# Expert weights in 18 places instead of 17, three of them loaded in the merge, and merged rows split into two halves per token tile

## The chip, the cores and the metric

The kernel runs on one core of a Trainium2 chip. The metric is the device time of one execution in microseconds (us), as the median of several executions. The engines are TensorE (PE, its weight loads PEld), VectorE (DVE), ScalarE (ACT), GpSimd (POOL) and SyncE (SP); SP issues nearly all plain DMAs, POOL the indirect ones.

## The reference

One decoder layer for 1024 tokens of 1024 channels in float32. A combined input projection feeds two token mixers (a native sparse attention with 8 heads and an attention over a latent with 8 heads). Their outputs are projected, merged with per-channel gates, projected once more and added to the input; a layer norm gives `h`. Then every token goes to two of 32 experts, and a second layer norm ends the layer.

```python
g_sel = argmax(h @ w_grp + b_grp)                  # one of 4 groups
e_logits = (h @ w_rtr + b_rtr)[group g_sel]        # 8 experts in it
top_l, top_i = lax.top_k(e_logits, 2)
...
y = (silu(x @ w_gate[e]) * (x @ w_up[e])) @ w_down[e]
out = layer_norm(ALPHA * h + sum of weight * y, ln2_g, ln2_b)
```

D_MODEL is 1024, the inner width of an expert 256, so an expert's three matrices are 3 MB in float32, and all 32 are 96 MB.

## The kernel before

**Precision.** Every float32 operand of a matmul is split into a high and a low part of a shorter type (`split`, lines 59 and 60: ACT casts the high part, DVE subtracts it for the low part), and three matmuls high*high, high*low, low*high stand for one.

**Stages.** Input projections (line 204); attention, head by head (lines 465 to 660); the merge (`merge_part`, line 711: for each block `dt` of 128 output channels, PE multiplies the two mixers' outputs by `w_br`, DVE multiplies by the gate, line 715, and adds the two, line 752); the output projection (line 978, eight tiles of 128 tokens, each followed by its layer norm, its router logits and the store of `h` into `h_d`); the routing tail, which makes the table `tkv` of the tokens of each expert; 32 experts, one after the other; the final norm.

**Before, merged rows.** For each `dt` the sum of line 752 is 128 channels by 1024 tokens. It is split at once into `MH`, four pairs of a high and a low tile with 256 tokens each. They lie in slots 9 to 16 of 8 KB a partition, all eight slots, and stay there until the output projection has read them as stationary operands.

**Slots.** On-chip memory is kept as numbered slots of 8 KB a partition, whose tiles take turns. Expert weights come in 96 loads of 1 MB (128 partitions by 8 KB) through `prefetch`, line 813; each load takes the next place of the list `RING`, 17 places in turn with `last` as the seventeenth. 16 loads are called for between the tiles of the output projection, when the places of `MH` come free, the others when an earlier expert has used its place. From load 18 on, a load waits until the load four before it has landed:

```python
            if n >= 18:
                tc.add_manual_dep(d, loads[n - 4].name, sync, reason="few loads in flight")
```

SP issues in the order of its instruction list; behind the 17th load it reads `novi` (line 1161), which the routing tail makes, and only then goes on.

**An expert** (class `Expert`, line 1020 on) takes a gather of its tokens from `h_d` (POOL, lines 1043 and 1046), eight transposes of them (`turn`, line 1063) and their split, four `up` steps (line 1086, each with a weight tile of 128x1024 split by `parts`, lines 1073 and 1074: ACT casts, DVE subtracts), SiLU times the second half (`act`, lines 1091 and 1092), a transpose (`flip`, line 1097), two `down` steps (line 1109, with two more split weight tiles), the scaling with the routing weight (ACT line 1112, DVE line 1113), and an indirect add into `acc_d` (POOL, line 1114). The six split weight tiles of an expert go in turn through slots 18, 19 and 20. PE's order in the experts is written by hand; the order of ACT, DVE, POOL and SP is decided when the kernel is built, by a scheduler with its own estimates of time. A moved address or load can therefore change the order of instructions elsewhere.

Of the kernel before, what the change touches and what calls it, by code (L numbers as in the profile page):

```python
# [18 lines left out]
P = 128  # L19
T = 1024  # L20
D = 1024
# [23 lines left out]
def layer_kernel(ctx: ExitStack, tc: tile.TileContext, A, out, dbg=None):  # L45
# [12 lines left out]
    def split(h, l, src):  # L58
        S.copy(h, src)  # L59
        V.tensor_tensor(l, src, f(h), op=ALU.subtract)  # L60
# [379 lines left out]
    def slot(j, shape, dt=F32):  # L440
        return (u1 if j < 5 else u3 if j < 7 else u2).tile(shape, dt, name=f"slot{j}", tag=f"slot{j}")
# [290 lines left out]
    aw0s.close()  # L732
    ats.close()

    hp = ctx.enter_context(tc.tile_pool(name="hp", bufs=1))
    u2 = ctx.enter_context(tc.tile_pool(name="u2", bufs=1))
    rp = ctx.enter_context(tc.tile_pool(name="rp", bufs=1, side="right"))
    with tc.tile_pool(name="mg", bufs=1, side="right") as mg:
        MH = [(slot(9 + 2 * q, [P, KD, 256], F32R), slot(10 + 2 * q, [P, KD, 256], F32R)) for q in range(4)]
        merge_part("a", 0)  # L740
        merge_weights(1, rp)
        merge_weights(2, rp)
        merge_part("b", 0)
        for dt in range(KD):
            if dt + 1 < KD:
                merge_part("a", dt + 1)
            if dt > 0:
                merge_part("b", dt)
            if dt + 3 < KD:
                merge_weights(dt + 3, rp)  # L750
            ga, gb = GV["a"].pop(0), GV["b"].pop(0)
            V.tensor_tensor(ga, ga, gb, op=ALU.add)
            for q in range(4):
                split(MH[q][0][:, dt], MH[q][1][:, dt], ga[:, q * 256:(q + 1) * 256])


    tkv = hp.tile([P, NE, 2], I32, name="tkv")
# [18 lines left out]
    def normalize(r, gb, pool, kind, nb, junk):  # L776
# [18 lines left out]
        else:  # L795
            S.activation(r, r, AF.Identity, scale=rs, bias=mv[:, 1:2])
            V.tensor_tensor(r, r, gb[:, 0], op=ALU.mult)
            (V if kind in "xy" else G).tensor_tensor(r, r, gb[:, 1], op=ALU.add)


    RING = [5, 6, 7, 7, 17, 9, 10, 11, 12, 13, 14, 15, 16, 1, 2, 0]
    weights, loads = [], []
    sync = mybir.DependencyInfo(mybir.DependencyClass.Sync, mybir.DependencyReason.DATA)

    def prefetch(n=1):
        for _ in range(min(n, 3 * NE - len(weights))):
            e, c = divmod(len(weights), 3)
            n = len(weights)
            if n == 2:
                pair["x"] = u0.tile([P, 2, 2, D], F32, name="ring7", tag="slot7")  # L810
            r = n % 17
            t = pair["x"][:, r - 2] if r in (2, 3) else ep.tile([P, 2, D], F32, name="last", bufs=1) if r == 16 else slot(RING[r], [P, 2, D])
            d = nc.sync.dma_start(flat(t), A["w_ex"][TURN[e], :, c * 2048:(c + 1) * 2048]).ins
            if n >= 18:
                tc.add_manual_dep(d, loads[n - 4].name, sync, reason="few loads in flight")
            loads.append(d)
            weights.append(t)

    with tc.tile_pool(name="wo", bufs=1, side="right") as wo, tc.tile_pool(name="wo2", bufs=2, side="right") as wo2:
        WO = []  # L820
# [146 lines left out]
        for i in range(NT):  # L967
            ts = slice(i * P, (i + 1) * P)
            s = ps.tile([P, T], F32, name="s")
            last = i == NT - 1  # L970
            xr = rp.tile([P, D], F32, name="wr", bufs=3)
            nc.sync.dma_start(xr, A["x"][ts])
            bs = wo2.tile([P, 2, 6], F32, name="bs")
            for cs in ((0,), (1,)) if last else ((0, 1),):
                for k in range(KD):
                    for x, (a, b) in enumerate(((0, 0), (0, 1), (1, 0))):
                        for c in cs:
                            mm = PE.matmul(s[:, HALF[c]], MH[i // 2][a][:, k, (i % 2) * P:(i % 2) * P + P],  # L978
                                           WO[k][:, b, HALF[c]], start=(k == 0 and x == 0),
                                           stop=(k == KD - 1 and x == 2)).ins  # L980
                cc = slice(512 * cs[0], 512 * cs[-1] + 512)
                V.scalar_tensor_tensor(xr[:, cc], xr[:, cc], ALPHA, s[:, cc], op0=ALU.mult, op1=ALU.add)
                for c in cs:
                    V.bn_stats(bs[:, c], xr[:, HALF[c]])
            mv, rs = moments(bs, wo2, 2)
            if last:
                with tc.issue_after(mm):
                    logits(hT, lt, range(KD))
                held = gather(i - 1, lt)
            hT = wo2.tile([P, T], F32, name="hT", bufs=1)  # L990
            lt = ps.tile([P, 512], F32, name="pt")
            for cs in ((0,), (1,)) if last else ((0, 1),):
                cc = slice(512 * cs[0], 512 * cs[-1] + 512)
                with tc.issue_after(done) if cs == (1,) else nullcontext():
                    done = scale(xr[:, cc], gb1[:, :, cc], mv, rs)
                for c in cs:
                    t = transposed([xr[:, k * P:(k + 1) * P] for k in range(4 * c, 4 * c + 4)])
                    S.copy(hT[:, HALF[c]], t)
            if i != NT - 2:
                logits(hT, lt, range(KD))  # L1000
            nc.sync.dma_start(h_d[ts], xr)
            kept.append(nc.sync.dma_start(acc_d[ts], xr).ins)
            if last:
                with tc.issue_after(done):
                    route(*held)
            if i != NT - 2:
                g = gather(i, lt)
                if g:
                    route(*g)
            prefetch({0: 5, 1: 2, 3: 2, 5: 2, 7: 5}.get(i, 0))  # L1010


        pp = ps.tile([P, 512], F32, name="pv")[:, 0:32]
# [148 lines left out]
    with tc.For_i(0, nov, 1) as j:  # L1162
# [10 lines left out]
        x.fetch()  # L1173
        x.turn()
        for c in range(3):
            x.w[c] = slot(RING[9 + c], [P, 2, D])
            nc.sync.dma_start(flat(x.w[c]), src[:, c * 2048:(c + 1) * 2048])
            if c < 2:
                x.up(4 * c)
                x.up(4 * c + 2)  # L1180
# [2 lines left out]
        x.down()  # L1183


    gb2 = slot(RING[8], [P, 2, D])
    for x, n in enumerate(("ln2_g", "ln2_b")):
        d = nc.sync.dma_start(gb2[:, x], A[n].partition_broadcast(P)).ins
        tc.add_manual_dep(d, loads[-1].name, sync, reason="not ahead of the experts")
    junk = slot(RING[9], [P, 2, D])[:, 0]  # L1190
    R = [t[:, x] for t in (slot(j, [P, 2, D]) for j in RING[4:8]) for x in range(2)]
    for i in range(NT):
        d = nc.sync.dma_start(R[i], acc_d[i * P:(i + 1) * P]).ins
        for o in Expert.sums:
# [96 lines left out]
def _program(shapes, extra=None):  # L1291
    import concourse.bacc as bacc

    nc = bacc.Bacc("TRN2", target_bir_lowering=False, num_devices=1)
    A = {n: nc.dram_tensor(f"in_{n}_dram", a.shape, mybir.dt.from_np(a.dtype), kind="ExternalInput").ap()
         for n, a in shapes.items()}
    out = nc.dram_tensor("out_0_dram", (T, D), F32, kind="ExternalOutput").ap()
    dbg = {n: nc.dram_tensor("dbg_" + n, s, mybir.dt.from_np(np.dtype(d)), kind="ExternalOutput").ap()
           for n, (s, d) in (extra or {}).items()}
    with tile.TileContext(nc, schedule_with_timeline_sim=True) as tc:  # L1300
        layer_kernel(tc, A, out, dbg)
    return nc
# [9 lines left out]
```

## Time and profile before

| what | value |
|---|---|
| median of 3 executions | 1442.29 us (1439.94 to 1443.75) |
| the profiled execution | 1442.7 us, span 1440.9 us |
| mean granted TensorE clock | 0.966 of full speed |
| PE / PEld / DVE busy | 1330.8 / 1099.4 / 1120.3 us |
| ACT / POOL busy | 764.8 / 457.6 us |
| DMA | 261.36 MB, mean 181 GB/s |

The span goes from the first to the last instruction; 1.8 us of the profiled execution's time lie around it. Times are in us from the span's start. Input projections fill 0 to 435, attention 435 to 820, the passage into the merge 820 to 845, the merge 845 to 925, the output projection 925 to 1018, the routing tail 1018 to 1060, the experts 1060 to 1395, and the final norm 1395 to 1441. "A <- B" in a view of waits is engine A idle until B's instruction was done.

### The profile page before, as it was taken

Reading aid. Unit: us, or ns where it says so; the run is one execution under the profiler, and the core shown is the slowest. Engines: PE = TensorE matmul, PEld = TensorE weight load, DVE = VectorE, ACT = ScalarE, POOL = GpSimd, SP = SyncE. Lnnn points to the kernel's source line nnn. Section 1 sums busy time; section 2 is a strip of 40 time slices with the busy share of each in tenths; the row PEclk is TensorE's granted clock in tenths of the full one; section 3 lists DMA queues with packets and bytes.
Section 4 is the critical chain, followed back from the end, with each engine's and each line's share of the span. In section 5 each row is a group of like instructions: output and inputs, shape, how many; then the busy total and the mean of one; then the engine's idle time right before and its main releaser. Section 6 shows DMA issues by size and latency. Waiting matters only on the chain.

```text
span 1440.9 us, 20097 instructions
## 1 busy us (share of the span) xinstructions
PE 1330.8 (92%) x6795; PEld 1099.4 (76%) x6795; DVE 1120.3 (78%) x2276; ACT 764.8 (53%) x1388; POOL 457.6 (32%) x457
## 2 busy tenths in 40 slices
PE   8999999999999999989999999999869999998950
PEld 8878888888887878878788778888757877776730
DVE  4323699889997878788889956654869999998946
ACT  4323323322117887778789732300248888877734
POOL 1112323312213344454444200002344444443315
PEclk9999999999998999999999999999979999999975
DMA  6023333497423332823521334765659999999834
GB/s 226 15 80 132 112 133 141 156 279 263 154 89 116 96 85 73 220 77 93 147 66 38 123 148 163 289 222 195 237 194 337 348 330 316 318 336 331 289 96 192
DMA packets 69476, 261.36 MB, mean 181 GB/s; under 512 B 15091, under 2 KB 16973, under 8 KB 57084
## 3 DMA queue, kind: packets, MB, share of 16 engines
q1 hardware_dynamic: 59644, 243.24, 48.9%
q0 software_dynamic: 9728, 16.82, 5.0%
q8 instruction: 54, 0.88, 0.3%
q14 instruction: 50, 0.41, 0.1%
HBM read 219.19 MB, written 70.70 MB: 201 GB/s over the span
## 4 chain that ended last, share of the span: by engine, by line
PE 60%; issue 16%; POOL 12%; DVE 5%; ACT 4%; DMA 2%; POOLq 0%; SPq 0%; DVEq 0%; ACTq 0%
PE s L204 24%; PE s L711 6%; PE s L978 6%; PE pt L490 5%; POOL acc_d L1114 5%; PE pv L546 3%; PE pv L545 3%; POOL xg L1046 2%; POOL xg L1043 2%; PE s L573 2%; PE pv L393 1%; PE s L574 1%; ACT pw L484 1%; PE s L652 1%; PE s L651 1%
## 5 line engine op out<-in xcount | busy, mean ns | idle before, releaser
L1086 PE MATMUL pt<-slot,slot 128*128 128x512 f32 x768 | 198.8, 405 | 11.9 <-DVE slot L1074 5.5
L1074 DVE TENSOR_TENSOR slot<-slot,slot 128x1024 fp32r<-128x1024 f32 x158 | 189.0, 1221 | 16.0 <-ACT slot L1073 10.0
L1073 ACT CAST slot<-slot 128x1024 fp32r<-128x1024 f32 x158 | 163.8, 1049 | 37.0 <-PE pt L1086 24.6
L1086 PEld LDWEIGHTS pt<-slot,slot 128*128 128x128 f32 x768 | 141.1, 190 | 51.6 <-DVE slot L1074 10.0
L186 POOL TENSOR_TENSOR wl<-wr,wh 128x1024 fp32r<-128x1024 f32 x39 | 95.0, 2438 | 262.0 <-ACT wh L185 262.0
L324 DVE TENSOR_SCALAR_CACHE_REDUCE jk<-idx,cand 128x384 bf16<-128x384 f32 (+1 forms) x186 | 164.4, 942 | 1.2
L60 DVE TENSOR_TENSOR ptl<-pt,pth 128x512 fp32r<-128x512 f32 (+1 forms) x240 | 148.3, 639 | 20.6 <-ACT pth L59 19.6
L59 ACT CAST pth<-pt 128x512 fp32r<-128x512 f32 (+1 forms) x240 | 128.5, 549 | 52.5 <-PE pt L490 44.3
L204 PE MATMUL s<-xh,wh 128*128 128x512 f32 x496 | 154.1, 391 | 2.3 <-DVE wi L168 1.4
L204 PE MATMUL s<-xh,wl 128*128 128x512 f32 x496 | 154.0, 390 | 0.0
L204 PE MATMUL s<-xl,wh 128*128 128x512 f32 x496 | 153.6, 389 | 0.0
L465 POOL TENSOR_SCALAR pb<-pb,st 128x128 f32<-128x128 f32 (+3 forms) x120 | 92.1, 786 | 183.4 <-DVE st L658 61.0
L185 ACT CAST wh<-wr 128x1024 fp32r<-128x1024 f32 x39 | 41.0, 1051 | 190.3 <-PE s L204 86.5
L1114 POOL DMA_INDIRECT acc_d<-wr,tkv x32 | 76.2, 2382 | 138.6 <-DVE wr L1113 138.6
L204 PEld LDWEIGHTS s<-xh,wh 128*128 128x128 f32 x496 | 92.2, 188 | 22.7 <-issue 2.6
L204 PEld LDWEIGHTS s<-xl,wh 128*128 128x128 f32 x496 | 93.1, 188 | 19.3
L204 PEld LDWEIGHTS s<-xh,wl 128*128 128x128 f32 x496 | 93.0, 188 | 19.2
L484 ACT ACTIVATE pb<-pb,st 128x128 f32<-128x128 f32 (+7 forms) x128 | 99.7, 780 | 12.0 <-DVE st L482 11.2
L1109 PE MATMUL s<-slot,hT 128*128 128x512 f32 x384 | 100.8, 408 | 2.0 <-DVE hT L60 1.5
L490 PE MATMUL pt<-ident,pb 128*128 128x128 f32 x576 | 92.7, 282 | 2.0 <-POOL pb L465 1.4
L978 PE MATMUL s<-slot,slot 128*128 128x512 f32 x384 | 93.3, 398 | 0.0
L1109 PEld LDWEIGHTS s<-slot,hT 128*128 128x128 f32 x384 | 70.5, 191 | 27.0 <-DVE hT L60 9.7
(345 smaller groups left out, 2932.5 us busy)
## 6 DMA issues: line engine op xcount, KB each, us to landing
slot<-in_w_ex_dram SPq DMA_DIRECT2D x79, 1024.0 KB
wr<-in_w_tt_dram SPq DMA_DIRECT2D x31, 512.0 KB
ring<-in_w_ex_dram SPq DMA_DIRECT2D x12, 1024.0 KB
b_d<-r_d SPq DMA_DIRECT2D x16, 576.0 KB
xw<-in_xw_dram SPq DMA_DIRECT2D x8, 718.0 KB
last<-in_w_ex_dram SPq DMA_DIRECT2D x5, 1024.0 KB
z_ga<-sh SPq DMA_DIRECT2D x8, 512.0 KB
slot<-b_d SPq DMA_DIRECT2D x8, 512.0 KB
```

Of the source, the lines that this page charges most:

```text
L59: S.copy(h, src)
L60: V.tensor_tensor(l, src, f(h), op=ALU.subtract)
L204: PE.matmul(z[:, c], w[:, k * P:(k + 1) * P], xx[:, k, c], start=(k == 0 and w is wh and xx is xh), stop=(k == KD - 1 and w is wl))
L324: V.tensor_scalar(jk[:, :n], idx[:, OFF[i]:OFF[i] + n], t, None, op0=op, op1=ALU.add, accum_out=cnt[:, i - 2:i - 1])
L484: S.activation(p, p, AF.Exp, bias=st[:, 0, j:j + 1], scale=-1.0, accum_out=st[:, 1, j:j + 1])
L490: PE.transpose(t[:rows, x * P:(x + 1) * P], c, ident)
L978: mm = PE.matmul(s[:, HALF[c]], MH[i // 2][a][:, k, (i % 2) * P:(i % 2) * P + P], WO[k][:, b, HALF[c]], start=(k == 0 and x == 0), stop=(k ...
L1073: S.copy(w[:, 0], self.w[k2 // 4][:, k2 % 4 // 2])
L1074: d = V.tensor_tensor(w[:, 1], self.w[k2 // 4][:, k2 % 4 // 2], f(w[:, 0]), op=ALU.subtract).ins
L1086: PE.matmul(self.a, self.xt[:, a, k * P:(k + 1) * P], w[:, b, (k - k2) * 512:(k - k2 + 1) * 512], start=(k == 0 and x == 0), stop=(k == KD ...
L1109: PE.matmul(s[:, c], self.hT[:, a, k * P:(k + 1) * P], w[:, b, c], start=(k == 0 and x == 0), stop=(k == 1 and x == 2))
L1114: d = G.indirect_dma_start(out=acc_d, out_offset=bass.IndirectOffsetOnAxis(ap=self.tok, axis=0), in_=y, in_offset=None, bounds_check=T - 1 ...
```

## The change

The merged rows are kept unsplit: line 752 becomes four adds of 128x256, straight into four tiles `MH` in slots 9 to 12. A token tile of 128 is split just for the output projection, in `MS`, slots 13 and 14 in turn: tile 0 during the merge, one 128x128 piece per `dt`; tile i+1 in the loop of the output projection ahead of tile i's matmuls. Slots 15 and 16 are free in the merge, and a new slot 21 exists, because the scratch memory for the descriptors of POOL's indirect DMAs is 8 KB a partition instead of 16. `RING` has 18 places and is written with its names. The first three loads (15, 16, 21) are called for at the start of the merge; the rule of four in flight begins at load 18 as before.

```diff
+    RING = [15, 16, 21, 5, 6, "a", "b", 17, 9, 10, 11, 12, 13, 14, 1, 2, 0, "last"]
...
+            if n >= len(RING):
+                tc.add_manual_dep(d, loads[n - 4].name, sync, reason="few loads in flight")
...
-        MH = [(slot(9 + 2 * q, [P, KD, 256], F32R), slot(10 + 2 * q, [P, KD, 256], F32R)) for q in range(4)]
+        MH = [slot(9 + q, [P, KD, 256]) for q in range(4)]
+        prefetch(3)
...
-            V.tensor_tensor(ga, ga, gb, op=ALU.add)
             for q in range(4):
-                split(MH[q][0][:, dt], MH[q][1][:, dt], ga[:, q * 256:(q + 1) * 256])
+                V.tensor_tensor(MH[q][:, dt], ga[:, q * 256:(q + 1) * 256], gb[:, q * 256:(q + 1) * 256], op=ALU.add)
+            if dt == 0:
+                MS[0] = slot(13, [P, 2, KD, P], F32R)
+            split(MS[0][:, 0, dt], MS[0][:, 1, dt], MH[0][:, dt, 0:P])
...
-    RING = [5, 6, 7, 7, 17, 9, 10, 11, 12, 13, 14, 15, 16, 1, 2, 0]
...
-            if n >= 18:
-                tc.add_manual_dep(d, loads[n - 4].name, sync, reason="few loads in flight")
...
+            if i + 1 < NT:
+                MS[i + 1] = slot(13 + (i + 1) % 2, [P, 2, KD, P], F32R)
+                split(MS[i + 1][:, 0], MS[i + 1][:, 1], MH[(i + 1) // 2][:, :, (i + 1) % 2 * P:(i + 1) % 2 * P + P])
...
-                            mm = PE.matmul(s[:, HALF[c]], MH[i // 2][a][:, k, (i % 2) * P:(i % 2) * P + P],
-                                           WO[k][:, b, HALF[c]], start=(k == 0 and x == 0),
+                            mm = PE.matmul(s[:, HALF[c]], MS[i][:, a, k], WO[k][:, b, HALF[c]], start=(k == 0 and x == 0),
...
-            prefetch({0: 5, 1: 2, 3: 2, 5: 2, 7: 5}.get(i, 0))
+            prefetch({0: 6, 2: 1, 4: 1, 6: 1, 7: 5}.get(i, 0))
...
-    nc = bacc.Bacc("TRN2", target_bir_lowering=False, num_devices=1)
+    nc = bacc.Bacc("TRN2", target_bir_lowering=False, num_devices=1, dynamic_dma_scratch_size=8192)
```

The other lines of the diff only name the same places by their new position in `RING` (a 33rd block that is rarely needed, the final norm's buffers).

**Where it moves instructions, 1: SP at the start of the merge.** `in_w_br` is a block of merge weights, `z_ga` and `z_gb` are stored gates, `o_b2` is a stored mixer output, `in_w_ex` the expert weights. Before:

```order
L714 DMA ga_9004<-z_ga2_85 128x1024
L714 DMA gb_9032<-z_gb1_92 128x1024
L694 DMA wr_8627<-o_b2_105 128x1024
L700 DMA wr_9035<-in_w_br_dram 128x1024
L700 DMA wr_9105<-in_w_br_dram 128x1024
L714 DMA gb_9102<-z_gb2_93 128x1024
L700 DMA wr_9175<-in_w_br_dram 128x1024
L714 DMA ga_9074<-z_ga3_86 128x1024
```

In the changed kernel:

```order
L694 DMA wr_8627<-o_b2_105 128x1024
L752 DMA slot15_8867<-in_w_ex_dram 128x2048
L752 DMA slot16_8869<-in_w_ex_dram 128x2048
L752 DMA slot21_8871<-in_w_ex_dram 128x2048
L700 DMA wr_9035<-in_w_br_dram 128x1024
L700 DMA wr_9102<-in_w_br_dram 128x1024
L700 DMA wr_9169<-in_w_br_dram 128x1024
L714 DMA ga_9071<-z_ga3_86 128x1024
L714 DMA gb_9099<-z_gb2_93 128x1024
```

Three loads of 1 MB stand ahead of the merge weights, and the third block of merge weights now stands ahead of the gate `z_gb2`.

**2: DVE in the output projection**, around the end of tile 1 (`wr` is the tile's rows, `s` its product, `bs` its norm's sums). Before:

```order
L982 SCALAR_TENSOR_TENSOR wr_9597<-wr_9597,s_9596 128x1024
L984 BN_STATS bs_9599<-wr_9597 128x6 x2
L766 BN_AGGR mv_9651<-bs_9599 128x2
L768 TENSOR_SCALAR rs_9653<-mv_9651 128x1
L773 SCALAR_TENSOR_TENSOR wr_9597<-wr_9597,mv_9651,gb1_9479 128x1024
```

In the changed kernel:

```order
L991 SCALAR_TENSOR_TENSOR wr_9584<-wr_9584,s_9580 128x1024
L60 TENSOR_TENSOR slot14_9762<-slot10_8864,slot14_9762 128x1024
L993 BN_STATS bs_9586<-wr_9584 128x6 x2
L792 BN_AGGR mv_9638<-bs_9586 128x2
L794 TENSOR_SCALAR rs_9640<-mv_9638 128x1
L799 SCALAR_TENSOR_TENSOR wr_9584<-wr_9584,mv_9638,gb1_9458 128x1024
```

The split of tile 3 comes right behind the read of tile 1's product, so one tile before PE needs it.

**3: ACT in the late experts.** `hh` is SiLU, `hT` and `slot3` or `slot4` are the splits of `flip` and `turn`, `wr` the scaling, the others weight casts into slots 18, 19 and 20. In most experts of both kernels the row of an expert reads 18, 19, 20, `hT`, `slot3`, 18, 19, `wr`, 20, `hh`. Before, expert 23 (behind the `hh` of expert 22), the first that differs:

```order
L1073 CAST slot19_12819<-slot5_12375 128x1024
L1073 CAST slot18_12809<-ring7_9591 128x1024
L1073 CAST slot20_12828<-slot5_12375 128x1024
L59 CAST hT_12794<-pv_12791 128x256
L59 CAST slot3_12806<-s_12797 128x1024
L1073 CAST slot18_12849<-ring7_9591 128x1024
L1112 ACTIVATE wr_12837<-s_12818,tkv_9427 128x512
L1091 ACTIVATE hh_12858<-pt_12772 128x256
L1073 CAST slot19_12867<-slot17_12469 128x1024
L1073 CAST slot20_12876<-slot17_12469 128x1024
```

In the changed kernel the first that differs is expert 24, and behind it comes expert 25:

```order
L1082 CAST slot18_12899<-slot16_12467 128x1024
L1082 CAST slot19_12909<-last_12375 128x1024
L1082 CAST slot20_12918<-last_12375 128x1024
L59 CAST hT_12884<-pv_12881 128x256
L59 CAST slot4_12896<-s_12887 128x1024
L1082 CAST slot18_12939<-slot16_12467 128x1024
L1121 ACTIVATE wr_12927<-s_12908,tkv_9406 128x512
L1100 ACTIVATE hh_12948<-pt_12862 128x256
L1082 CAST slot19_12957<-slot5_12559 128x1024
L1082 CAST slot20_12966<-slot5_12559 128x1024
L1082 CAST slot19_13003<-slot21_12469 128x1024
```

Call the form in which both late casts (19 and 20) stand behind `hh` form A, and one in which they stand between `wr` and `hh` form B. Before, experts 23, 24 and 27 have form A, 26 and 30 form B, and all five cast 19 ahead of 18 at their start. In the changed kernel, experts 24 and 27 have form A, and 25, 26 and 30 form B; expert 24 casts 18 first.

The addresses that move change the order in the first half of attention too, on all engines; in the second half, the routing tail and the final norm the order is the same as before.

## Rows read from the trace of the kernel before

**Rows 1.** The page: engine busy time over the span, and the granted clock in 40 slices.

```profile
PE 1330.8 (92%) x6795; PEld 1099.4 (76%) x6795; DVE 1120.3 (78%) x2276; ACT 764.8 (53%) x1388; POOL 457.6 (32%) x457
PEclk9999999999998999999999999999979999999975
```

**Rows 2.** Windows: length, PE, PEld, DVE, ACT, POOL busy, clock, DMA share, GB/s.

```profile
435.00:625.00 190.00, 178.70 (x1124) 153.53 (x1124) 151.31 (x453) 151.00 (x393) 82.98 (x134) 0.96 0.43 121
625.00:820.00 195.00, 189.74 (x1227) 160.28 (x1225) 173.07 (x460) 161.00 (x394) 77.56 (x118) 1.00 0.27 78
...
845.00:925.00 80.00, 80.00 (x341) 64.17 (x341) 51.40 (x64) 23.98 (x43) 0.00 (x0) 0.99 0.52 176
925.00:1018.00 93.00, 93.00 (x476) 77.52 (x475) 49.11 (x138) 8.61 (x20) 13.40 (x13) 1.00 0.63 234
1018.00:1060.00 42.00, 28.23 (x158) 24.11 (x156) 31.45 (x135) 7.03 (x12) 21.29 (x20) 0.74 0.63 233
...
1210.00:1260.00 50.00, 50.00 (x239) 39.69 (x238) 49.04 (x53) 42.56 (x53) 23.99 (x17) 1.00 0.96 318
...
1300.00:1360.00 60.00, 53.58 (x246) 40.56 (x245) 52.13 (x55) 44.01 (x55) 22.72 (x15) 1.00 0.96 331
```

**Rows 3.** The chain that ended last: start us, length us, what; one row per expert here.

```profile
1080.95 2.51 POOL acc_d L1114
...
1283.50 2.50 POOL acc_d L1114
...
1293.81 1.58 POOL acc_d L1114
...
1306.67 1.58 POOL acc_d L1114
...
1383.91 2.47 POOL acc_d L1114
```

**Rows 4.** Timeline of ACT, end of expert 22 and in 23: start, length, what, idle.

```profile
1283.17 0.39 ACT L1091 ACTIVATE hh<-pt 128x256 f32<-128x256 f32 x1
1284.46 1.05 ACT L1073 CAST slot<-slot 128x1024 fp32r<-128x1024 f32 x1 [0.90 <-PE pt L1086]
...
1292.05 0.69 ACT L1112 ACTIVATE wr<-s,tkv 128x512 f32<-128x512 f32 x1 [1.81 <-PE s L1109]
```

**Rows 5.** Waits, 1284 to 1400: engine, line, for whom, total us, times, longest.

```profile
PE pt L1086 <- DVE slot L1074: 5.5, 10, 0.6
PE pt L1086 <- ACT slot L1073: 4.9, 5, 1.4
```

**Rows 6.** Timeline of SP: the first and the last of 21 weight loads in a row.

```profile
1187.91 0.33 SPq L813 DMA_DIRECT2D slot<-in_w_ex_dram  x1
...
1267.80 0.33 SPq L813 DMA_DIRECT2D ring<-in_w_ex_dram  x1
```

**Rows 7.** Groups by line, 845 to 925: names, shapes, count, busy us, mean ns, idle before.

```profile
L60 DVE TENSOR_TENSOR slot<-wr,slot 128x1024 fp32r<-128x1024 f32 x15 | 18.1, 1218 | 2.8 <-ACT slot L59 2.8
L59 ACT CAST slot<-wr 128x1024 fp32r<-128x1024 f32 x15 | 15.6, 1050 | 41.7 <-issue 19.2 <-PE s L711 15.9 <-DMA wr<-in_w_out_dram 5.8
L60 DVE TENSOR_TENSOR slot<-ga,slot 128x256 fp32r<-128x256 f32 x28 | 10.0, 418 | 1.9 <-ACT slot L59 1.9
...
L752 DVE TENSOR_TENSOR ga<-ga,gb 128x1024 f32<-128x1024 f32 x7 | 8.5, 1219 | 0.0
```

**Rows 8.** Timelines of SP and of DVE in the merge: gate `z_gb2` requested, and used.

```profile
850.52 0.33 SPq L714 DMA_DIRECT2D gb<-z_gb  x1
...
874.60 1.22 DVE L715 TENSOR_TENSOR gb<-s,gb 128x1024 f32<-128x1024 f32 x1 [4.38 <-PE s L711]
```

**Rows 9.** The page: the queue of indirect DMAs, and the scatters of the experts.

```profile
q0 software_dynamic: 9728, 16.82, 5.0%
...
L1114 POOL DMA_INDIRECT acc_d<-wr,tkv x32 | 76.2, 2382 | 138.6 <-DVE wr L1113 138.6
```

**Rows 10.** Waits of PE, 435 to 625, the longest.

```profile
PE pv L546 <- DVE ptl L60: 2.6, 2, 2.1
```

More of the change, by code (lines that the diff above doesn't have):

```diff
@@ L733, in layer_kernel, with prefetch @@
     ats.close()
+    RING = [15, 16, 21, 5, 6, "a", "b", 17, 9, 10, 11, 12, 13, 14, 1, 2, 0, "last"]
+    weights, loads = [], []
+    sync = mybir.DependencyInfo(mybir.DependencyClass.Sync, mybir.DependencyReason.DATA)
+    MS = {}
+    def prefetch(n=1):
+        for _ in range(min(n, 3 * NE - len(weights))):
+            n = len(weights)
+            e, c = divmod(n, 3)
+            r = RING[n % len(RING)]
+            if r == "a" and n < len(RING):
+                pair["x"] = u0.tile([P, 2, 2, D], F32, name="ring7", tag="slot7")
+            if r == "last":
+                t = ep.tile([P, 2, D], F32, name="last", bufs=1)
+            else:
+                t = pair["x"][:, "ab".index(r)] if r in ("a", "b") else slot(r, [P, 2, D])
+            d = nc.sync.dma_start(flat(t), A["w_ex"][TURN[e], :, c * 2048:(c + 1) * 2048]).ins
+            if n >= len(RING):
+                tc.add_manual_dep(d, loads[n - 4].name, sync, reason="few loads in flight")
+            loads.append(d)
+            weights.append(t)
     hp = ctx.enter_context(tc.tile_pool(name="hp", bufs=1))
@@ L798, in normalize @@
             (V if kind in "xy" else G).tensor_tensor(r, r, gb[:, 1], op=ALU.add)
-    RING = [5, 6, 7, 7, 17, 9, 10, 11, 12, 13, 14, 15, 16, 1, 2, 0]
[L802 to L813, printed above, removed]
-            if n >= 18:
-                tc.add_manual_dep(d, loads[n - 4].name, sync, reason="few loads in flight")
-            loads.append(d)
-            weights.append(t)
     with tc.tile_pool(name="wo", bufs=1, side="right") as wo, tc.tile_pool(name="wo2", bufs=2, side="right") as wo2:
@@ L1175, in layer_kernel @@
         for c in range(3):
-            x.w[c] = slot(RING[9 + c], [P, 2, D])
+            x.w[c] = slot(RING[14 + c], [P, 2, D])
             nc.sync.dma_start(flat(x.w[c]), src[:, c * 2048:(c + 1) * 2048])
@@ L1183, in layer_kernel @@
         x.down()
-    gb2 = slot(RING[8], [P, 2, D])
+    gb2 = slot(RING[12], [P, 2, D])
     for x, n in enumerate(("ln2_g", "ln2_b")):
@@ L1189, in layer_kernel @@
         tc.add_manual_dep(d, loads[-1].name, sync, reason="not ahead of the experts")
-    junk = slot(RING[9], [P, 2, D])[:, 0]
-    R = [t[:, x] for t in (slot(j, [P, 2, D]) for j in RING[4:8]) for x in range(2)]
+    junk = slot(RING[13], [P, 2, D])[:, 0]
+    R = [t[:, x] for t in (slot(j, [P, 2, D]) for j in RING[8:12]) for x in range(2)]
     for i in range(NT):
```

## The prediction

> **What bounds the kernel now.** I read the page first. PE works in 92% of the span and its granted clock is at the upper of its two levels (2.4 GHz) nearly everywhere [rows 1], so a gain has to come from a stretch in which PE idles, or a loss from a stretch that becomes one. The windows by stage [rows 2] tell which. In the merge and the output projection, where most of the edits lie, PE is busy 80.00 of 80 us and 93.00 of 93; DVE has 51.40 and 49.11 us of work there, ACT 23.98 and 8.61. Both stages are PE's. In the experts there are two regimes. From 1210 to 1260 PE is busy 50.00 of 50 us and DVE 49.04. From 1300 to 1360 PE has only 53.58 of 60.
>
> The chain of waits dates this [rows 3]. The adds into `acc_d` come 21 experts apart at 1080.95 and 1283.50, so one expert takes 202.55 / 21 = 9.65 us. From there to 1383.91 it takes 100.41 us for nine experts where 9 x 9.65 = 86.85 would do: **13.56 us are lost in the last ten experts.** The timeline of ACT shows where [rows 4]. Behind the `hh` of expert 22 ACT goes on, but in expert 23 it stands at `wr`, line 1112, for 1.81 us until PE's down step is done, and only behind the `hh` after it can it cast the two weight tiles that PE wants. PE waits for these casts and DVE's subtractions, 4.9 and 5.5 us in the longest rows [rows 5], and for no DMA. So those experts are bound by the order in which ACT and DVE were told to work (form A and form B of the section on the change), not by late weights.
>
> **The change, part by part.**
>
> *Merge.* Removed for each `dt`: one add of 128x1024, 1.22 us on DVE, and four splits of 128x256, 4 x 0.42 = 1.7 us on DVE by the row's mean [rows 7]. Added: four adds of 128x256 and one split of 128x128. The row nearest to such an add is the 128x256 subtraction, 0.42 us, so the adds take 1.7 us and the small split no more than 0.42. DVE ends 0.8 us per `dt` cheaper and ACT three casts lighter, in a stage in which PE is never idle: 0. If that cover were gone, 8 x 0.8 = 6 us would be DVE's gain alone.
>
> *Three loads in the merge.* SP now issues 3 MB ahead of three blocks of merge weights and the gate `z_gb2`. What queues behind them is late by at most their transfer. A load of 1 MB takes 4.0 us in the weight stage: 20 loads lie between 1187.91 and 1267.80 [rows 6]. So 12 us, and 6 us more for the three blocks of 0.5 MB now ahead of the gate and the gate `z_ga3`, at the same rate, rounded up to four half loads' 8 us. Before, `z_gb2` was requested at 850.52 and used at 874.60 [rows 8], 24 us later; 12 + 8 = 20 us still fits, and the stage's DMA share is 0.52 [rows 2]. The first of them also waits until the last attention head has left its memory. I take 0; at the upper end 2 us, if DVE takes the gate late and PE waits for its product's buffer.
>
> *Output projection.* Seven splits of 128x1024 come in: 7 x 1.05 us on ACT, 7 x 1.22 on DVE [rows 7]. ACT goes from 8.61 to 16 us of 93, DVE from 49.11 to 57.7 [rows 2]. They stand one tile of 93 / 8 = 11.6 us ahead of PE's need (the second pair of order rows), so PE does not wait: 0. They delay each tile's norm and store of `h` by 1.2 us, but there is none behind the last two tiles, with which the routing tail begins: 0. The upper end is one split in front of PE, 1.05 + 1.22 = 2.3 us.
>
> *Descriptor scratch.* The queue of the indirect DMAs is busy 5.0% of the span, and the scatters take POOL 2.38 us each, 76.2 us in all, in which POOL is not the bound: it idles 138.6 us in front of them [rows 9]. I take 0. What a full ring costs no row shows. The Trainium skill ("SBUF — State Buffer", section "SBUF size: 192, 224, or 256?") says that 16 KiB a partition are set aside as the ring of descriptors that GpSimd writes; half of it would speak against the change, and no run here shows how much of the ring is in use.
>
> *One place more.* SP has 18 loads ahead of its wait for `novi` where it had 17: one load, 4.0 us by the rate above, is done earlier. PE waits for no load in the last experts [rows 5], so that is lead, not time: 0 here, and the price of a rival below.
>
> *Order of the late experts.* This is the term with a sign. Form A costs what the step from 1293.81 to 1306.67 costs over the regular one: 12.86 - 9.65 = 3.2 us [rows 3]. Before, there were three of form A and two of form B, 13.56 us in all, so B is (13.56 - 9.6) / 2 = 2.0 us. The changed kernel has two of A and three of B. Four of them keep their swapped first casts: 3.2 + 3 x 2.0 = 9.2. The fifth, expert 24, is an A without the swap; it lies between 2.0 and 3.2, and I take 2.6, the middle. That makes 11.8 against 13.56: **-1.8 us** (-1.2 to -2.4).
>
> *First half of attention.* The order changes there on every engine, with the same instructions. PE idles 190.00 - 178.70 = 11.3 us in 435 to 625 and 195.00 - 189.74 = 5.3 us in 625 to 820 [rows 2]; the longest single wait on PE's list is 2.1 us [rows 10]. If the new order loses as little as the second half does, it gains 6.0 us; by mirror, I allow 6.0 us of loss. Nothing on the rows tells the sign: I take 0.
>
> **The sum** is -1.8 us on the profiled execution's 1442.7, so 1440.9. The median of the runs is 0.4 us lower than that execution; on the median's footing it is **1440.5 us**. A measurement of this kernel can tell about 0.3%, 4.3 us, from no change, so this forecast reads as no change.
>
> **Rivals.**
>
> *1. The weights bind: faster.* In 1210 to 1260 the DMA share is 0.96 at 318 GB/s [rows 2], and three loads of 4.0 us are 12.0 us per expert, more than PE's 9.65. Whoever reads the stage as bound by DMA gives each load spared 4.0 us; with the order's 1.8 that is 5.8 us, 1436.5. The Trainium skill ("DMA: Bandwidth & Descriptors", section "Specifications") puts the limit of HBM for one core at about 358 GB/s. By that limit a load of 1.05 MB is 2.9 us, an estimate, and three of them are 8.8 us, so the stage would be a little below PE's 9.65; the trace's 318 GB/s stays under the limit. For this rival speaks that the lead must shrink by 12.0 - 9.65 = 2.35 us per expert. Against it, no row has PE, ACT or DVE behind a weight DMA [rows 5]. The late forms of ACT's order give the supply 13.56 us of pause, about what the last nine experts would fall behind by (9 x 2.35 = 21 us) less the lead that they start with. In the changed kernel the pause is 1.8 us shorter and the lead 4.0 us longer, so still no bind. Chance 0.13.
>
> *2. The new order of attention is better: faster.* -6.0 - 1.8 = -7.8 us, 1434.5. Chance 0.15.
>
> *3. The new order of attention is worse: slower.* One more hole on PE between 435 and 625 that lets its clock fall: the mean clock is 0.96 there, against 1.00 in the second half [rows 2]. If the new order opens as much idle time again as the second half has (5.3 us), and the clock costs another 0.04 x 190 = 7.6 us at most, the loss is 5.3 to 12.9 us; with the middle, 9.1, and -1.8 it is +7.3, 1449.6. It decides when PE's idle time in that stretch passes 11.3 + 6.1 = 17.4 us. Against it: the work is the same and PE waits in pieces of 2.1 us at most. Chance 0.17.
>
> *4. The smaller ring holds the adds.* If an add were held by its own 2.38 us again, 32 x 2.38 = 76 us would lie beside 138.6 us of POOL's idle time [rows 9]; it would count only where adds end the stage, for the last two experts, 2 x 2.38 = 4.8 us: 1442.3 - 1.8 + 4.8 = 1445.3. Chance 0.04.
>
> *5. The change does not bring its place early.* If the first load in the merge has to wait for memory until the output projection, the lead is no longer than before. By the first term nothing is lost: 1440.5. This is inside the forecast.
>
> **How the numbers follow.** The forecast with its small terms (order of the late experts -2.4 to -1.2, attention within 2.5 either way) has 0.51, rival 4 has 0.04, and both lie within 0.3%: 0.55. Rivals 1 and 2 have 0.28 and lie on the faster side beyond it, rival 3 has 0.17 on the slower. The predicted time is that of the forecast, 1440.5. The range runs from 1434.0, which takes in rivals 1 and 2 at their prices, to 1446.5, which is the forecast with the whole 6.0 us of loss in attention; what is left out is most of rival 3, and a better attention together with weights that bind. The forecast's own range is 1438 to 1443.
>
> **What would show it.** In the profile of the changed kernel: one expert still 9.65 us up to about expert 22; from expert 23 to 30 about 11.8 us lost in five long steps, with the first at 24; PE busy 80 of 80 in the merge and 93 of 93 in the output projection; three weight loads near 846; no wait of PE on a weight DMA; PE's idle time in 435 to 625 near 11 us. It is wrong if the regular expert gets shorter than 9.65 us or the late loss falls under 8 us (then the weights did bind), if the attention half moves by over 2.5 us, or if PE idles in the merge.

## The result

The changed kernel takes 1436.1 us in the median of 16 runs against 1442.54 for the kernel before: a ratio of 0.9949, 95% interval 0.9939 to 0.996. That is 0.5% faster, 6.4 us by the medians. The forecast was 1440.5 and its range 1434.0 to 1446.5; the time lies in the range, but below the 1438 to 1443 that the prediction gave to the forecast itself, on the side that had a chance of 0.28.

The profiled execution took 1435.09 us with a span of 1433.3. The page of the changed kernel, the lines that answer to [rows 1]:

```profile
PE 1331.3 (93%) x6779; PEld 1098.3 (77%) x6795; DVE 1116.7 (78%) x2283; ACT 763.0 (53%) x1371; POOL 458.1 (32%) x457
PEclk9999999999998999999999999999969999999985
```

PE has as much work as before in a shorter span. The windows of the changed kernel in the same stretches as [rows 2], with the same columns:

```profile
435.00:625.00 190.00, 181.66 (x1142) 155.15 (x1147) 153.08 (x460) 153.11 (x399) 81.37 (x127) 0.97 0.43 121
625.00:820.00 195.00, 189.40 (x1214) 159.87 (x1224) 173.31 (x462) 160.90 (x393) 80.07 (x124) 1.00 0.27 81
...
845.00:925.00 80.00, 80.00 (x347) 64.77 (x346) 46.20 (x70) 15.75 (x21) 0.21 (x2) 1.00 0.61 221
925.00:1018.00 93.00, 93.00 (x478) 77.28 (x477) 54.58 (x143) 13.60 (x22) 13.19 (x12) 1.00 0.56 206
1018.00:1060.00 42.00, 27.79 (x149) 23.53 (x147) 30.07 (x131) 7.03 (x12) 22.65 (x21) 0.70 0.62 225
...
1210.00:1260.00 50.00, 50.00 (x239) 39.91 (x238) 48.92 (x53) 42.39 (x53) 22.45 (x15) 1.00 0.96 316
...
1300.00:1360.00 60.00, 53.88 (x238) 40.36 (x239) 49.89 (x52) 41.91 (x53) 21.28 (x14) 0.97 0.92 314
```

Merge and output projection are full on PE as before; DVE and ACT have less work in the one and more in the other, as forecast (in the output projection DVE has 54.58 us, where 57.7 were costed). The idle time of PE in 435 to 625 falls from 11.3 to 190.00 - 181.66 = 8.3 us. The late experts lose as much as before. The span is 7.6 us shorter, so more than half of that is not in these rows. The table takes single instructions of PE and SP out of the two traces and shows where it is:

| stretch | before, us | after, us | difference |
|---|---|---|---|
| start to the merge's first matmul (line 711 before) | 821.50 | 818.89 | -2.6 |
| from there to the first expert's `turn` | 235.45 | 234.76 | -0.7 |
| from there to the `flip` of expert 21 | 219.06 | 218.89 | -0.2 |
| `flip` of 21 to `flip` of 31 | 109.32 | 109.09 | -0.2 |
| `flip` of 31 to the issue of the last store | 48.12 | 47.80 | -0.3 |
| the last store's issue to the end | 7.41 | 3.77 | **-3.6** |

The last row is a place that no part of the prediction speaks of. The timelines of POOL and SP at the end of the kernel before (start, length, instruction, idle before):

```profile
1430.17 3.25 POOL L798 TENSOR_TENSOR slot<-slot,slot 128x1024 f32<-128x1024 f32 x1 [2.30 <-DVE slot L797]
...
1424.91 8.87 SPq L1198 DMA_DIRECT2D out_dram<-slot  x4
```

And of the changed kernel:

```profile
1426.15 3.25 POOL L824 TENSOR_TENSOR slot<-slot,slot 128x1024 f32<-128x1024 f32 x1 [2.30 <-DVE slot L823]
...
1427.23 2.53 SPq L1207 DMA_DIRECT2D out_dram<-slot  x2
```

Before, POOL's last instruction ends at 1433.42 and the span at 1440.9; now it ends at 1429.40 and the span at 1433.3. Between them stand only the last store and the closing barrier, at which all engines wait for each other. Ahead of it each engine has a `DRAIN`, an instruction of its sequencer that is not counted as busy time. The records of POOL's `DRAIN` at the end of the program (ns of the shortest, the median and the longest; starts of the first and the last), before:

```profile
L1300 POOLq DRAIN  x3: 46/109/9925, 1430.1 to 1440.6; - x3
```

And in the changed kernel:

```profile
L1309 POOLq DRAIN  x3: 46/109/5062, 1426.1 to 1433.0; - x3
```

The longest is the first. Before, it starts with POOL's last instruction, at 1430.14, and ends at 1440.06, 6.6 us after that instruction, while SP is through with its stores at 1436.4. In the changed kernel it takes 5.06 us and ends at 1431.17, 1.8 us after POOL's last instruction, and SP comes to the barrier last, at 1432.4. So before, the program's end waits for POOL's `DRAIN`; after the change it waits for the last store.

### The profile page after: what moved, and what is told of

Read it like the earlier page. It is cut to its first block, busy times and chain, and to the rows that moved or that the text cites. A ratio compares the mean times of both kernels' runs of the same rounds, so it can differ in the third digit from the quotient of the medians.

```text
span 1433.3 us, 20049 instructions
## 1 busy us (share of the span) xinstructions
PE 1331.3 (93%) x6779; PEld 1098.3 (77%) x6795; DVE 1116.7 (78%) x2283; ACT 763.0 (53%) x1371; POOL 458.1 (32%) x457
```

## The experiments

Three theories stood after the result. **S**: the smaller scratch makes the end shorter and moves addresses, which gives attention another order; the places and loads bring nothing yet. **P**: the eighteenth place and the loads in the merge bring lead, and lead is time. **O**: the form of the late experts' order decides.

**1 and 2. Both kernels once more.** No edit; only a profile each.

> The kernel before once more, unchanged, for how far a stage moves by itself. In the first pair of profiles the last stretch, from the last flip to the end, took 55.5 us before and 51.6 after the change, though no instruction of it changed its order. If that is chance, this run can show anything from 51 to 56 there; if the change's other addresses cause it, it shows 55 to 56 again. The merge should begin near 821.5 us (within 0.7) if the 2.6 us gained ahead of it belong to the new order of attention, and anywhere between 818 and 822 if they are chance. The steps of the late experts should repeat within 0.2 us each.

> The changed kernel once more, unchanged. If the order of attention is what brought 2.6 us, the merge begins near 818.9 us again (within 0.7). The step of 14.36 us between two flips (expert 27, form A), in which the clock fell to its lower level for some 3 us, repeats if form A as such invites it, and is 12.9 us as in the kernel before if it was chance. Last stretch: 51 to 52 if the change causes it, up to 56 if it is chance.

Measured: the kernel before has its merge at 823.5 and the last store 7.40 us ahead of the end; the changed kernel 819.3 and 3.76. The steps of the late experts repeat: 12.87, 12.85, 9.53, 11.78 and 12.87 us from expert 23 on before; in the changed kernel the step at expert 27 is 14.42 us again, but the step at expert 24 takes 13.55 us instead of 12.10. The expectation that the last stretch repeats if it belongs to the change holds (55.4 and 51.4). The merge of the unchanged kernel was expected within 0.7 us of 821.5, and came 2.0 later: its begin moves by that much on its own, so its 2.6 us are less certain than the end's 3.6.

**3 and 4. ACT and DVE in a hand-written order from expert 16 on**, on either kernel:

```diff
+            if e == 16:
+                hand = ExitStack()
+                hand.enter_context(tc.manual_schedule(engines={mybir.EngineType.Activation, mybir.EngineType.DVE}))
             ex[e].up(0)
             ex[e].up(2)
+            if e >= 16:
+                ex[e].parts(4)
+                ex[e - 1].parts(8)
+                ex[e - 1].parts(10)
...
+            if e >= 16:
+                ex[e].parts(6)
             ex[e].up(4)
+            if e >= 16 and e + 1 < NE:
+                ex[e + 1].parts(0)
             if e > 0:
                 ex[e - 1].down()
                 prefetch(3)
+            if e >= 16 and e + 1 < NE:
+                ex[e + 1].parts(2)
             ex[e].up(6)
             ex[e].act()
```

> The kernel before with one edit: from expert 16 on ACT and DVE too follow an order written by hand, the one of the regular experts, so that forms A and B are gone; 17 places as before. Theory (the late loss is all order): 13.7 us of long steps vanish, so about 1429. Rival (the weights were about to bind): with steps of 9.65 us the lead over the loads shrinks by 2.35 us per expert and 10 us of it are used up about expert 27, so PE waits for weights in the last ones and only 2 to 5 us are gained, 1438 to 1440.

> The changed kernel with the same hand-written order from expert 16 on; 18 places. Theory (order alone): the late loss of 13.4 us vanishes, about 1423, so it gains as much over the changed kernel as the same edit gains over the kernel before. Rival (the weights bind once the order does not): the one load more of lead, 4.0 us, is now worth its time, so this kernel gains some 4 us more than the same edit on the kernel before, about 1428 to 1431.

Measured: 1442.08 us on the kernel before, ratio 0.9997 (0.9988 to 1.0006), so nothing; 1428.7 on the changed kernel, ratio 0.9903 (0.9887 to 0.9918) to the kernel before. The first is the rival's outcome, and gains even less than the rival's 2 to 5 us. With the forms gone, experts run at 9.65 us up to expert 25 with 17 places and up to 26 with 18, and then wait for weights. The waits of ACT on DMA in the kernel before with this order, 1275 to 1392:

```profile
ACT slot L1073 <- DMA slot<-in_w_ex_dram: 9.7, 5, 3.2
ACT slot L1073 <- DMA ring<-in_w_ex_dram: 1.5, 1, 1.5
ACT slot L1073 <- DMA last<-in_w_ex_dram: 1.2, 1, 1.2
```

And in the changed kernel with it:

```profile
ACT slot L1082 <- DMA slot<-in_w_ex_dram: 11.9, 7, 3.1
```

ACT stands 12 us at weight loads in both, where no such row existed before. So forms A and B hid a limit that was due anyway: **the weights come at 4.0 us a load (20 loads between 1188.1 and 1268.2 us with 17 places), 12.0 an expert, and the lead is used up.** In these two profiles the `flip`s of 21 and 31 are 102.40 and 102.49 us apart, alike; but from the last `flip` to the last store's issue it is 50.6 us with 17 places and 47.9 with 18, 2.7 us that expert 31 waits longer for its last weights. That is of the size of the one load's 4.0 us. The medians differ by more than that and the end's 3.6 us. The profile with 17 places is the fastest of its 11 executions (1438.05 us, the median 1442.08), so a usual execution loses more than these rows show; where, no trace shows. Runs 8 and 9 below take the comparison further.

**5. Only the scratch.** The kernel before with 8 KB:

```diff
-    nc = bacc.Bacc("TRN2", target_bir_lowering=False, num_devices=1)
+    nc = bacc.Bacc("TRN2", target_bir_lowering=False, num_devices=1, dynamic_dma_scratch_size=8192)
```

> The kernel before with one edit: 8 KB of descriptor scratch instead of 16; merged rows, places and loads as before. By its instruction order it has the changed kernel's attention, and late experts with four steps of form A (23, 24, 25, 28). Theory now: from the last store's issue to the end 7.4 us shrink to about 3.8, attention brings 2.6 us, the late order 1 to 2 us: about 1435 to 1436, the whole gain of the change. Rival (the gain is the place more and the loads in the merge): 1440 to 1442.

Measured: 1436.83 us, ratio 0.996 (0.9946 to 0.9973), where the whole change has 0.9949 (0.9939 to 0.996). One line of the diff gives the gain within the intervals: theory S. In its profile the merge begins at 819.4, from there to the first `turn` it is 234.6 us, and the last store stands 3.76 us ahead of the end. The 0.7 us between merge and experts, which I had put to the merge's edits after run 2, are there with no edit in the merge.

**6 and 7. Everything but the scratch.** The changed kernel with 16 KB, hence without slot 21; the second time for its profile:

```diff
-    RING = [15, 16, 21, 5, 6, "a", "b", 17, 9, 10, 11, 12, 13, 14, 1, 2, 0, "last"]
+    RING = [15, 16, 5, 6, "a", "b", 17, 9, 10, 11, 12, 13, 14, 1, 2, 0, "last"]
...
-        prefetch(3)
+        prefetch(2)
...
-    nc = bacc.Bacc("TRN2", target_bir_lowering=False, num_devices=1, dynamic_dma_scratch_size=8192)
+    nc = bacc.Bacc("TRN2", target_bir_lowering=False, num_devices=1)
```

> The changed kernel without slot 21 and with 16 KB of scratch: rows unsplit, two loads in the merge, 17 places. Its attention has the order of the kernel before, its late experts two steps of form A and two of B with one more A at 23, as before. Theory: only the 0.7 us of the merge are left, about 1441.5, and the last store's issue stands 7.4 us ahead of the end again. Rival (unsplit rows and early loads are what pays): 1436 to 1438.

> The changed kernel without slot 21 and with 16 KB of scratch once more, for its profile. Theory: merge begins at 821 to 823.5 us, the merge and the output projection last as long as in the kernel before within 0.1 us each though the rows are split elsewhere and two loads run beside the merge, and the last store's issue stands 7.4 us ahead of the end: about 1442.

Measured: 1442.2 us, ratio 0.9995 (0.9986 to 1.0004): nothing. The profile has the merge at 822.1, 235.7 us from it to the first `turn`, and 7.41 us behind the last store. The unsplit rows, their splits in the output projection and two loads beside the merge cost and bring nothing, as the prediction's first three terms said.

**8. No loads in the merge.** The changed kernel, its first three loads held behind the output projection's first rows:

```diff
-        prefetch(3)
...
-            nc.sync.dma_start(xr, A["x"][ts])
+            xd = nc.sync.dma_start(xr, A["x"][ts]).ins
+            if i == 0:
+                with tc.issue_after(xd):
+                    prefetch(3)
```

> The changed kernel with its first three loads held back until the first rows of the output projection have been asked for, so that none runs in the merge; 18 places, 8 KB. Theory: PE does not wait for weights until the late experts and all 18 places are still full when the experts begin, so the same as the changed kernel, 1436 within 1 us. Rival (early loads are lead that pays): 4 to 12 us slower, 1440 or more.

Measured: 1435.96 us, ratio 0.9944 (0.993 to 0.9959), the same as with the loads in the merge. In either case SP issues 18 loads ahead of its wait for `novi`, the last of them at 1035.5 us with the early loads and at 1037.7 without, where the merge began 2.6 us later. So the early loads bring no lead in this order.

**9. The scratch alone with the hand-written order**, the edits of 3 and 5 together; 17 places.

> The kernel before with 8 KB of scratch and with the hand-written order of ACT and DVE from expert 16 on; 17 places. The same hand-written order brought 0.2 us on the kernel before and 7.4 us on the changed one. If the place more is what makes it pay (the weights bind with 17), this stays at 1434 to 1436, the scratch's gain alone. If the place more has no part in it, it comes near the changed kernel with the same order, 1428.7, within 1.5 us.

Measured: 1435.95 us, ratio 0.9953 (0.9938 to 0.9968), against 0.996 with the scratch alone. With 17 places the hand-written order brings next to nothing, on 16 KB and on 8; with 18 it brings 0.9949 - 0.9903 = 0.46%, 6.6 us. So what the changed kernel has beside the scratch counts once the order stops hiding the weights: theory P, but only there. That it is the place more, and not the unsplit rows or the early loads, is argued from runs 6 to 8, which show nothing for those in the old order; the hand-written order with the place alone was not run. How much it brings is open, too: the medians of 9 and 4 are 7.2 us apart, their profiles (spans of 1428.4 and 1427.8, with merges that begin at 817.8 and 820.1) only 610.6 - 607.7 = 2.9 us behind the merge's begin. One load is 4.0 us. The profile of run 9 is again its fastest execution (1430.15 us of six, the median 1435.95), that of run 4 lies near its median (1429.59), so the two profiles show less of the difference than the medians.

**10. 8 KB of scratch with nothing moved.** The kernel before, 8 KB, and the free 8 KB held by an unused tile, so that PE and ACT keep the order of the kernel before:

```diff
+    pad = ctx.enter_context(tc.tile_pool(name="pad", bufs=1, side="left")).tile([P, 2048], F32, name="pad")
+    nc.gpsimd.memset(pad[:, 0:1], 0.0)
```

> The kernel before with 8 KB of descriptor scratch, and the 8 KB that come free held by a tile that nothing uses (one tiny memset writes into it), so that every other address and the order of PE and ACT stay those of the kernel before. Theory (the smaller scratch shortens the program's end by itself, and the rest is the new order of attention): the last store's issue stands 3.8 us ahead of the end instead of 7.4, the merge begins at 821 to 823.5 as before, and the median falls by 3.6 us, to about 1438.6. Rival (the end follows from other addresses or another order): 7.4 us again and no change, 1442.2.

Measured: 1440.11 us, ratio 0.9977 (0.9964 to 0.9991), which is 3.3 us. The end of its timelines of POOL and SP, with a span of 1440.6:

```profile
1433.51 3.25 POOL L800 TENSOR_TENSOR slot<-slot,slot 128x1024 f32<-128x1024 f32 x1 [2.30 <-DVE slot L799]
...
1428.25 8.87 SPq L1200 DMA_DIRECT2D out_dram<-slot  x4
```

POOL's last instruction ends at 1436.76, 3.8 us ahead of the span's end, where it was 1440.9 - 1433.42 = 7.5. POOL's `DRAIN`, in the same form as above:

```profile
L1302 POOLq DRAIN  x3: 46/109/5061, 1433.5 to 1440.3; - x3
```

ACT and DVE run the same instructions in the same order as in the kernel before, by the two traces, and POOL too but for the memset. The merge began at 825.2, and 236.0 us lie between it and the first `turn`: those parts did not get faster. So the end's share is shown by itself, 3.6 us in the profile, and what is left of the gain goes with the other addresses and the order that follows from them. No run parts these two, and the intervals of this run and of run 5 overlap.

**11. 12 KB of scratch.** As run 5, with 12288.

> The kernel before with 12 KB of scratch. Its instruction order is that of the run with 8 KB alone. Theory: attention gains the 2.6 us (merge begins near 819.5) and the passage into the merge 0.75; the end is in between: if GpSimd's 6.7 us from its last instruction to the closing barrier grow with the size of the scratch, they are about 5.0 here and the last store's issue stands 5.7 us ahead of the end: about 1438. Rival (the end has two states and no size): 7.4 or 3.8 us.

Measured: 1435.82 us, ratio 0.9947 (0.9929 to 0.9966); 5.04 us from the last store's issue to the end. Its end, with a span of 1438.3:

```profile
1429.88 3.25 POOL L798 TENSOR_TENSOR slot<-slot,slot 128x1024 f32<-128x1024 f32 x1 [2.30 <-DVE slot L797]
...
1427.61 5.88 SPq L1198 DMA_DIRECT2D out_dram<-slot  x3
```

```profile
L1300 POOLq DRAIN  x3: 46/109/7555, 1429.8 to 1438.0; - x3
```

1438.3 - 1433.13 = 5.2 us behind POOL's last instruction, between the 7.5 of 16 KB and the 3.9 of 8. POOL's `DRAIN` takes 9.93 us with 16 KB, 7.55 with 12 and 5.06 with 8, within 0.01 us in all thirteen profiles: 0.62 to 0.63 us for each KB. It does grow with the size, and the rival of two states is out. With 12 KB it still ends behind SP, at 1437.40 against 1436.1; with 8 KB it ends ahead of SP, so by these rows a scratch below 8 KB would bring this kernel's end nothing more; none was run. What POOL does in its `DRAIN` no record shows. The median was expected about 2 us higher; the profiled execution, with 1440.03, is the slowest of its six. The merge began at 822.9 in this profile, though, no earlier than before, while the passage of 234.8 us is that of the 8 KB kernels with the new order. Over all profiles with the new order of attention the merge begins at 817.8 to 823.0 (eight, mean 820.4), over those with the old at 821.2 to 825.2 (five, mean 822.7): 2.3 us, with spreads that overlap.

**12. Eight loads in flight** instead of four, on the changed kernel with the hand-written order:

```diff
-                tc.add_manual_dep(d, loads[n - 4].name, sync, reason="few loads in flight")
+                tc.add_manual_dep(d, loads[n - 8].name, sync, reason="few loads in flight")
```

> The changed kernel with the hand-written order from expert 16 on and eight weight loads in flight instead of four. In the profile of the hand-written order with four, the last experts still lose 6 us to waits for weights. If the rule of four limits the supply, loads come faster than one in 4.0 us and up to 6 us are gained, about 1423; if the DMA engines are full anyway (share 0.96 to 0.99), the same as with four, 1428.7 within 1.5 us.

Measured: 1429.85 us, ratio 0.9909 (0.989 to 0.9927): the same as with four within the intervals. In its profile the loads do come a little faster (338 GB/s in 1110 to 1310, where it is 327 with four), ACT waits 6.6 us for them instead of 11.9, and the `flip`s of 21 and 31 are 100.75 us apart instead of 102.49; but behind the last `flip` 1.2 us of that are lost again, and the time does not show the rest. The rule of four is at most a small part of the limit.

## Why the prediction was right or wrong

**The bound of each stage: right.** PE is busy 80.00 of 80 and 93.00 of 93 us again, one expert takes 9.65 us up to expert 23, and no load is waited for. In the changed kernel the first long step is at expert 24, as the order said.

**Merge, three loads, output projection: right, 0.** Runs 6 and 7 show it for the rows, their splits and two loads, run 8 for the three loads. The sizes too: the four adds take the time of the 128x256 subtraction, by the groups of the changed kernel, 845 to 925:

```profile
L59 ACT CAST slot<-wr 128x1024 fp32r<-128x1024 f32 x12 | 12.5, 1050 | 49.9 <-PE s L711 36.2 <-DMA wr<-in_w_out_dram 13.7
L777 DVE TENSOR_TENSOR slot<-ga,gb 128x256 f32<-128x256 f32 x32 | 11.4, 418 | 0.0
```

0.42 us each [rows 7]. The three loads were issued ahead of the merge weights, and the gates 7 us behind the first of them; `z_gb2` was requested at 849.06 and used at 871.23, 22 us later, where [rows 8] show 24. The timeline of SP in the changed kernel:

```profile
841.66 1.29 SPq L752 DMA_DIRECT2D slot<-in_w_ex_dram  x3
843.94 3.73 SPq L700 DMA_DIRECT2D wr<-in_w_br_dram  x3
848.68 0.33 SPq L714 DMA_DIRECT2D ga<-z_ga  x1
849.06 1.28 SPq L714 DMA_DIRECT2D gb<-z_gb  x1
```

**Descriptor scratch: wrong, and this is the step that failed.** The prediction took 0, since the queue of indirect DMAs is busy 5.0% of the span and POOL idles ahead of its adds, and asked only what a smaller ring could cost during the run. It gave 3.6 us at the program's end. The rows of before held it: POOL's last instruction ended 7.5 us ahead of the span's end, with one store between, and the prediction did not ask what ends the program. The passage of the Trainium skill cited beside it, that 16 KiB are set aside for these descriptors, was read as something that speaks against the change; with 8 KB no run is slower, and the experts' adds are as before (2.40 us each in the changed kernel, 2.38 before, and a regular step is 9.65 us with either size).

**Order of the late experts: the direction right, the gain taken back.** Forms A and B appear where the order put them, and in the first profile four of the five at their prices: B's steps take 11.78 us, 2.1 over the regular one, and the A without a swap 12.10, 2.5 over it, where 2.0 and 2.6 were expected. But the A at expert 27 took 14.36 us, not 12.86. The windows of this step, before and after, first the kernel before:

```profile
1332.70:1345.56 12.86, 10.36 (x47) 7.49 (x46) 10.75 (x12) 8.93 (x11) 4.29 (x3) 1.00 0.94 329
```

The changed kernel:

```profile
1315.70:1327.48 11.78, 10.36 (x48) 7.50 (x47) 9.53 (x11) 8.03 (x11) 5.30 (x3) 1.00 0.94 329
1327.48:1341.84 14.36, 11.85 (x48) 8.52 (x46) 11.87 (x12) 8.92 (x11) 4.30 (x3) 0.88 1.00 335
1341.84:1351.40 9.56, 9.56 (x47) 7.73 (x46) 8.05 (x9) 8.19 (x10) 4.15 (x3) 1.00 0.91 313
```

The granted clock falls to 0.88 in the mean, the lower level for a part of the step. It is the fourth long step in a row here, where the kernel before has two in a row at 1.00. But the number of long steps does not explain it. In the second profile of the changed kernel the clock also fell in the first long step, that of expert 24, with regular steps before it:

```profile
1292.32:1305.87 13.55, 11.62 (x47) 8.66 (x46) 9.44 (x11) 8.00 (x10) 3.92 (x4) 0.87 1.01 325
```

In runs 5 and 11 it fell in the third (13.31 and 13.38 us). The timeline of PE in the step of expert 27 in the first profile shows the price:

```profile
1333.68 1.56 PE L1095 MATMUL pt<-slot,slot 128*128 128x512 f32 x6
1336.64 0.73 PE L1095 MATMUL pt<-slot,slot 128*128 128x512 f32 x2 [1.41 <-ACT slot L1082]
1337.90 4.14 PE L1095 MATMUL pt<-slot,slot 128*128 128x512 f32 x10 [0.53 <-DVE slot L1083]
```

1.56 / 6 = 0.26 us a matmul ahead of the hole, 4.14 / 10 = 0.41 behind it. So the 1.8 us came and 1.5 went: 109.09 against 109.32 us between the `flip`s of 21 and 31. The five long steps lose 13.6 us over 9.65 us each, where 11.8 were forecast. The step of expert 27 repeats, 14.42 in run 2 and 14.17 in run 8; with the step of expert 24 as well, run 2 has 109.94 us between the two `flip`s, so there the whole 1.8 us and more went. Why the clock falls in these steps is open: no run changes that alone.

**First half of attention: inside its bounds, and not 0.** 2.3 us in the mean of all profiles, with spreads that overlap, and 0.8 us in the passage behind it, without overlap (234.6 to 234.9 us against 235.5 to 236.0), go with the new addresses and order. In the first pair of profiles it was 2.6 us, just over the 2.5 that the prediction had named as a sign of being wrong. Rival 2, with -6.0, had the sign.

**Rival 1, the weights bind: wrong for this change, right for the next.** Runs 3, 4 and 9 show that the working of its pause and lead was sound: without the 13.6 us of late order the supply binds from expert 26 on, and with the place more only from expert 27 on, which is 2.7 to 2.9 us in the profiles and more in the medians. Rivals 3 and 4 did not happen: PE's idle time in 435 to 625 fell, and no add became slower.

So the sum was off by two terms of opposite kind: the end's -3.6 and attention's -3.1 with the passage behind it were missing, the order's -1.8 was given back. That the time still fell into the range is luck: its lower end, 1434.0, was set by rivals 1 and 2, and over half of the 6.4 us came from the program's end, which no term or rival held.

## What to carry to other kernels

Read what lies between the last useful instruction and the end of the span, the sequencers' instructions too, before pricing anything that touches a queue's memory: here a build parameter by itself moved the closing barrier by 3.6 us and no stage at all. A change of sizes also moves addresses, and with a scheduler that orders by them it is two changes; holding the freed memory with an unused tile parts the two in one run. And an inefficiency that stands in front of a limit hides what the limit's remedy is worth: the place more paid nothing that the runs can tell while the order stood and, with the order mended, is part of a version at 1428.7 us, ratio 0.9903 to the kernel before, that beats both kernels.

## What the runs showed that was not expected

- POOL's `DRAIN` at the end of the program takes 9.93 us with 16 KB of descriptor scratch, 7.55 with 12 and 5.06 with 8. It starts with POOL's last instruction, of 3.25 us, and ends 6.6, 4.3 and 1.8 us behind it.
- The granted clock fell to 0.87 to 0.90 over single long steps of the late experts: the fourth in a row in three profiles of the changed kernel and its edit, the third in runs 5 and 11, and once the first. In the kernel before, with two in a row, it stayed at 1.00.
- Eight weight loads in flight instead of four brought 338 GB/s instead of 327 in 1110 to 1310, and no time that can be measured.
